# RMS norm and swish on one core: units of 8 rows in place of 4, and three pieces of work moved between engines

## The chip, the cores and the metric

The kernel runs on one core of a Trainium2 chip. The core has several engines, each with its own program: ScalarE (ACT in the profile), VectorE (DVE), GpSimd (POOL) and SyncE (SP) are used here; TensorE isn't. They work side by side and order themselves by semaphores. Data moves between the chip's memory (HBM) and the core's SBUF by DMA, which is started by an instruction on SyncE or ScalarE and then runs by itself on 16 DMA engines. [...]

The metric is the device time of one execution in microseconds. Before the change it is 161.33 us, the median of 3 runs from 159.96 to 161.42.

## The reference

```python
# x: 16 x 1024 x 512 float32; gamma: 512; eps = 1e-5
rms = np.sqrt(np.mean(x ** 2, axis=-1, keepdims=True) + eps)
x_norm = x / rms * gamma
return (x_norm * (1.0 / (1.0 + np.exp(-x_norm)))).astype(np.float32)
```

There are 16,384 rows of 512 numbers. Each row is scaled by one over its root mean square, multiplied by gamma, and passed through swish. 33.56 MB are read and as many written.

## The kernel before

**Rows and groups.** A "row" below means one row of x in each of the 128 partitions, so there are 128 of them, in four groups of 32. The buffer `xb` holds 96 rows; group 3 takes the place of group 0. All work on the rows is done in place. A load or store moves a piece of a group, given as (group, first row, rows).

**Loads** (line 117) are issued by SyncE in the order of the list `loads`. The first two are moved ahead of the start-up barrier (`early`). Loads of group 3 wait until the store of the piece that lay in the same place has landed.

**Stores** (line 191) are issued by ScalarE, inside its own program. A store waits for the swish of its last rows. `hold` makes stores 0 and 2 wait for a load as well, and gives the earliest place in ScalarE's program for them; so reads and writes mostly take turns: reads of groups 0 to 2, writes of group 0, reads of group 3, writes of groups 1 to 3.

**The work on a chunk of 4 rows**, k = 0 to 31:

- square(k), ScalarE: two row squares whose sum the engine accumulates itself (line 162, each followed by an instruction that reads the accumulator out), then one instruction that squares the other two rows into the PSUM buffer `sq` (line 169). A row square waits until the one two before it is done, by the semaphore `s_acc`.
- sums(k), VectorE: a reduction of `sq` to two row sums (line 215).
- GpSimd: adds eps (line 143) and raises to the power -0.5 (line 150).
- norm(k), VectorE: four instructions, each multiplies one row by its factor and by gamma (line 226).
- swish(k), ScalarE: one instruction over the four rows (line 181).

**The order on each engine is written out by hand.** ScalarE does square(k), then a store if one is due, then swish(k-2). VectorE does sums(k) and then norm(k-1). So norm(k-1) stands behind sums(k), which needs square(k), which may need a load.

At the start GpSimd clears three small tiles (lines 137 to 139). One of them is the buffer into which gamma is loaded; VectorE then spreads gamma over the partitions by a shuffle (line 239).

Of the kernel before, what the change touches and what calls it, by code (L numbers as in the profile page):

```python
# [9 lines left out]
def kernel(  # L10
# [7 lines left out]
    nc = tc.nc  # L18
    P = nc.NUM_PARTITIONS
    AF = mybir.ActivationFunctionType  # L20
    ALU = mybir.AluOpType
    fp32 = mybir.dt.float32
# [3 lines left out]
    R, D = xf.shape  # L26

    groups = [32] * 4
    slots = [0, 32, 64, 0]
    loads = [(0, 0, 4), (0, 4, 4), (0, 8, 8), (0, 16, 16), (1, 0, 32)]  # L30
    loads += [(2, 0, 28), (2, 28, 4), (3, 0, 28), (3, 28, 4)]
    stores = [(0, 0, 28), (0, 28, 4), (1, 0, 32), (2, 0, 32)]
    stores += [(3, 0, 16), (3, 16, 8), (3, 24, 8)]
    hold = {0: (loads.index((2, 0, 28)), 12), 2: (loads.index((3, 0, 28)), 22)}
    behind = {}
    ring = 96
    early = 2
    cn = 4
    n_sq = 2

    first = [sum(groups[:g]) for g in range(len(groups))]
    assert P * sum(groups) == R, R
# [1 line left out]

    chunks = []
    for i, (g, r, n) in enumerate(loads):
        for c in range(r, r + n, cn):
            chunks.append((slots[g] + c, i if c == r else None))
    K = len(chunks)
    assert K * cn * P == R  # L50

    ends = [-(-(first[g] + r + n) // cn) for g, r, n in stores]

    inv_d = 1.0 / float(D)
    eps_f = float(eps)
# [4 lines left out]
    def sbuf(name, shape, dt=fp32):  # L60
        return nc.alloc_sbuf_tensor(name, shape, dt).ap()

    xb = sbuf("xb", [P, ring, D])
    gamma4 = sbuf("gamma4", [P, D])
    gamma_sb = sbuf("gamma_sb", [P, D])
    neg_half = sbuf("neg_half", [P, cn])
    ms = sbuf("ms", [P, K, cn])
    aeps = sbuf("aeps", [P, K, cn])
    rstd = sbuf("rstd", [P, K, cn])
    sq = [nc.alloc_psum_tensor(f"sq{i}", [P, n_sq, D], fp32).ap() for i in range(2)]  # L70
    junk = [nc.alloc_psum_tensor(f"junk{i}", [P, D], fp32).ap() for i in range(2)]

    ld = [nc.alloc_semaphore(f"ld{t}") for t in range(len(loads))]
# [2 lines left out]
    blank = sbuf("blank", [P, 16])  # L76
    s_blank = nc.alloc_semaphore("s_blank")
    s_scratch = nc.alloc_semaphore("s_scratch")
    s_gld = nc.alloc_semaphore("s_gld")
    s_zero = nc.alloc_semaphore("s_zero")  # L80
    s_half = nc.alloc_semaphore("s_half")
    s_gamma = nc.alloc_semaphore("s_gamma")
    s_acc = nc.alloc_semaphore("s_acc")
    s_sq = nc.alloc_semaphore("s_sq")
    s_sum = nc.alloc_semaphore("s_sum")
    s_eps = nc.alloc_semaphore("s_eps")
    s_rstd = nc.alloc_semaphore("s_rstd")
    s_norm = nc.alloc_semaphore("s_norm")
    s_swish = nc.alloc_semaphore("s_swish")

    def need(ins, sem, value):
        return ins.wait_op(sem, value, "sem-ge")
# [30 lines left out]
    for t in range(early):  # L123
# [3 lines left out]
        at = next(  # L127
            i for i, other in enumerate(entry)
            if other.engine == mybir.EngineType.SP
            and isinstance(other, mybir.InstDrain)  # L130
        )
# [2 lines left out]
        load(t)  # L134
    nc.sync.wait_ge(s_scratch, 16)

    nc.gpsimd.memset(blank, 0.0).then_inc(s_blank, 1)  # L137
    nc.gpsimd.memset(gamma4, 0.0).then_inc(s_zero, 1)  # L138
    nc.gpsimd.memset(neg_half, -0.5).then_inc(s_half, 1)  # L139
    nc.gpsimd.wait_ge(s_half, 1)  # L140
    for k in range(K):
        need(
            nc.gpsimd.tensor_scalar(  # L143
                out=aeps[:, k, :], in0=ms[:, k, :], scalar1=eps_f, scalar2=None,
                op0=ALU.add,
            ),
            s_sum, k + 1,
        ).then_inc(s_eps, 1)
        need(
            nc.gpsimd.tensor_tensor(  # L150
                out=rstd[:, k, :], in0=aeps[:, k, :], in1=neg_half, op=ALU.pow
            ),
            s_eps, k + 1,
        ).then_inc(s_rstd, 1)

    def square(k):
        at, landing = chunks[k]
        if landing is not None:
            nc.scalar.wait_ge(ld[landing], 16)  # L159
        for j in range(n_sq, cn):  # L160
            n = k * (cn - n_sq) + j - n_sq
            acc = nc.scalar.activation(  # L162
                out=junk[n % 2], in_=xb[:, at + j, :], func=AF.Square,
                scale=inv_d**0.5, accum_out=ms[:, k, j : j + 1],
            )
            if n >= 2:
                need(acc, s_acc, n - 1)
            acc.then_inc(s_acc, 1)
        square = nc.scalar.activation(  # L169
            out=sq[k % 2], in_=xb[:, at : at + n_sq, :],  # L170
            func=AF.Square, scale=inv_d**0.5,
        )
        if k >= 2:
            need(square, s_sum, k - 1)
        square.then_inc(s_sq, 1)

    def swish(k):
        at, _ = chunks[k]
        rows = xb[:, at : at + cn, :]
        need(  # L180
            nc.scalar.activation(out=rows, in_=rows, func=AF.Silu), s_norm, k + 1  # L181
        ).then_inc(s_swish, 1)

    def after(t):
# [19 lines left out]
    for k in range(K + 3):  # L204
        if k < K:
            square(k)
        while stored < len(stores) and max(ends[stored] + 2, after(stored)) <= k:
            store(stored)
            stored += 1
        if 2 <= k < K + 2:  # L210
            swish(k - 2)

    def sums(k):
        need(
            nc.vector.tensor_reduce(  # L215
                out=ms[:, k, 0:n_sq], in_=sq[k % 2], op=ALU.add,
                axis=mybir.AxisListType.X,
            ),
            s_sq, k + 1,
        ).then_inc(s_sum, 1)  # L220

    def norm(k):
        at, _ = chunks[k]
        for j in range(cn):
            row = xb[:, at + j, :]
            ins = nc.vector.scalar_tensor_tensor(  # L226
                out=row, in0=row, scalar=rstd[:, k, j : j + 1], in1=gamma_sb,
                op0=ALU.mult, op1=ALU.mult,
            )
            if j == 0:  # L230
                need(ins, s_rstd, k + 1)
        ins.then_inc(s_norm, 1)

    for k in range(K + 1):
        if k < K:
            sums(k)
        if k == 0:
            need(
                nc.vector.stream_shuffle(gamma_sb, gamma4, [0] * 32), s_gld, 16  # L239
            ).then_inc(s_gamma, 1)  # L240
        if k == 1:
            nc.vector.wait_ge(s_gamma, 1)
        if k >= 1:
            norm(k - 1)
# [39 lines left out]
```

## Time and profile before

| What | Value |
|---|---|
| Median of 3 runs | 161.33 us |
| The profiled execution | 161.41 us |
| Its span in the profile | 160.1 us |
| Instructions in the span | 496 |
| Read, written | 33.56 MB, 33.56 MB |
| Mean transfer rate over the span | 419 GB/s |
| Busy: ScalarE, VectorE, GpSimd | 129.7, 124.4, 65.5 us |

The profile is of one execution. Its page gives the busy time of each engine, the span in 40 equal slices (each digit is a tenth of busy time, for DMA the mean share of the 16 DMA engines), the chain of work that ended last, and groups of like instructions. A line of a group reads: line of the kernel, engine, operation, output from inputs, shapes, count, then busy us in all and mean ns of one, then the idle time of the engine just before them, and what ended it. Longer views of the same trace list the instructions in order of time (start us, duration us, engine, line, operation) and the transfers that were issued in a stretch of time, with the us from issue to landing. "SPq" and "ACTq" mean the issuing of a transfer by SyncE or ScalarE.

### The profile page before, as it was taken

What the parts mean: (1) busy time and instruction counts of PE and PEld (TensorE: products, weight loads), DVE (VectorE), ACT (ScalarE), POOL (GpSimd) and SP (SyncE); (2) the same over time, 40 slices, a digit from 0 to 9 for tenths busy, and PEclk for the clock granted to TensorE, in tenths of its full rate; (3) what the DMA queues carried; (4) which work ended last, traced back from release to release, by engine and by line L of the source; (5) the groups of instructions that cost most, each with busy time, mean ns of one, the idle gap of its engine ahead of it and who ended that gap; (6) DMA issues with size and microseconds to landing.
All of it is one profiled execution on the core that took longest, in us unless ns stands there. A gap on an engine that the chain in (4) does not pass through costs nothing.

```text
span 160.1 us, 496 instructions
## 1 busy us (share of the span) xinstructions
DVE 124.4 (78%) x162; ACT 129.7 (81%) x193; POOL 65.5 (41%) x71
## 2 busy tenths in 40 slices
DVE  0239989999199998899999999999999999970000
ACT  0937989994799988999999999999999999571000
POOL 1035555555055555555555555555555555500000
DMA  7999996996999997999969996996996997899896
GB/s 264 458 461 393 450 598 262 524 524 262 458 461 446 444 411 338 458 458 458 450 258 458 458 458 266 518 524 278 508 508 297 508 475 327 385 426 483 368 426 270
DMA packets 2460, 67.16 MB, mean 419 GB/s; under 512 B 404, under 2 KB 404, under 8 KB 408
## 3 DMA queue, kind: packets, MB, share of 16 engines
q1 hardware_dynamic: 1296, 33.56, 49.4%
q10 hardware_dynamic: 1160, 33.57, 48.8%
q14 instruction: 4, 0.03, 0.0%
HBM read 33.56 MB, written 33.56 MB: 419 GB/s over the span
## 4 chain that ended last, share of the span: by engine, by line
ACT 55%; DMA 24%; DVE 7%; issue 3%; ACTq 1%; SPq 0%
ACT xb L181 24%; DMA xb<-in_x_dram 24%; ACT junk L162 18%; ACT sq L169 13%; DVE xb L226 5%; DVE ms L215 2%; ACTq L191 1%; SPq L117 0%; ACTq L159 0%
## 5 line engine op out<-in xcount | busy, mean ns | idle before, releaser
L226 DVE SCALAR_TENSOR_TENSOR xb<-xb,rstd,gamma_sb 128x512 f32<-128x512 f32 x128 | 87.3, 744 | 0.0
L181 ACT ACTIVATE xb<-xb 128x2048 f32<-128x2048 f32 x32 | 60.9, 1902 | 4.8 <-DVE xb L226 3.8
L215 DVE TENSOR_REDUCE ms<-sq 128x2 f32<-128x1024 f32 x32 | 39.2, 1223 | 16.1 <-ACT sq L169 13.1
L143 POOL TENSOR_SCALAR aeps<-ms 128x4 f32<-128x4 f32 x32 | 20.6, 644 | 70.0 <-DVE ms L215 70.0
L150 POOL TENSOR_TENSOR rstd<-aeps,neg_half 128x4 f32<-128x4 f32 x32 | 44.0, 1376 | 2.7
L162 ACT ACTIVATE junk<-xb 128x512 f32<-128x512 f32 x64 | 37.2, 582 | 6.7 <-DMA xb<-in_x_dram 6.6
L169 ACT ACTIVATE sq<-xb 128x1024 f32<-128x1024 f32 x32 | 32.1, 1005 | 0.0
L162 ACT ACTIVATION_READ_ACCUMULATOR junk<-xb 128x1 f32 x64 | 11.9, 186 | 0.0
L202 ACT ACT_TABLE_LOAD x1 | 1.3, 1283 | 3.6 <-issue 3.6
L239 DVE LOAD_MASK_SELECT gamma_sb<-gamma x1 | 0.0, 14 | 2.5 <-DMA gamma<-in_gamma_dram 2.5
L239 DVE STREAM_SHUFFLE gamma_sb<-gamma 128x512 f32<-128x512 f32 x1 | 0.7, 715 | 0.0
L137 POOL MEMSET blank<- 128x16 f32 x1 | 0.1, 111 | 1.5 <-POOLq L58 1.5
L138 POOL MEMSET gamma<- 128x512 f32 x1 | 0.5, 525 | 0.0
L265 POOL MEMSET const-float32-0.0<- 128x1 f32 x1 | 0.1, 98 | 0.2 <-issue 0.2
L265 POOL MEMSET const-bfloat16-1.0<- 128x1 bf16 x1 | 0.1, 102 | 0.0
L265 POOL MEMSET const-uint8-127<- 128x1 uint8 x1 | 0.1, 101 | 0.0
L139 POOL MEMSET neg_half<- 128x4 f32 x1 | 0.1, 101 | 0.0
L265 POOL MEMSET const-float32-1.0<- 128x1 f32 x1 | 0.1, 98 | 0.0
## 6 DMA issues: line engine op xcount, KB each, us to landing
xb<-in_x_dram SPq DMA_DIRECT2D x2, 7168.0 KB, 38.4
out_dram<-xb ACTq DMA_DIRECT2D x1, 7168.0 KB, 19.3
xb<-in_x_dram SPq DMA_DIRECT2D x4, 1024.0 KB, 14.0
xb<-in_x_dram SPq DMA_DIRECT2D x1, 4096.0 KB, 19.5
out_dram<-xb ACTq DMA_DIRECT2D x1, 4096.0 KB, 20.1
out_dram<-xb ACTq DMA_DIRECT2D x2, 2048.0 KB, 16.1
xb<-in_x_dram SPq DMA_DIRECT2D x1, 2048.0 KB, 10.2
out_dram<-xb ACTq DMA_DIRECT2D x1, 1024.0 KB, 21.3
```

What stands on the lines that cost most here:

```text
L138: nc.gpsimd.memset(gamma4, 0.0).then_inc(s_zero, 1)
L143: nc.gpsimd.tensor_scalar(out=aeps[:, k, :], in0=ms[:, k, :], scalar1=eps_f, scalar2=None, op0=ALU.add,),
L150: nc.gpsimd.tensor_tensor(out=rstd[:, k, :], in0=aeps[:, k, :], in1=neg_half, op=ALU.pow),
L162: acc = nc.scalar.activation(out=junk[n % 2], in_=xb[:, at + j, :], func=AF.Square, scale=inv_d**0.5, accum_out=ms[:, k, j : j + 1],)
L169: square = nc.scalar.activation(out=sq[k % 2], in_=xb[:, at : at + n_sq, :], func=AF.Square, scale=inv_d**0.5,)
L181: nc.scalar.activation(out=rows, in_=rows, func=AF.Silu), s_norm, k + 1
L191: nc.scalar.dma_start(out=dram(of, stores[t]), in_=buf(stores[t])),
L202: nc.scalar.preload_act_table_set("silu_and_others")
L215: nc.vector.tensor_reduce(out=ms[:, k, 0:n_sq], in_=sq[k % 2], op=ALU.add, axis=mybir.AxisListType.X,),
L226: ins = nc.vector.scalar_tensor_tensor(out=row, in0=row, scalar=rstd[:, k, j : j + 1], in1=gamma_sb, op0=ALU.mult, op1=ALU.mult,)
L239: nc.vector.stream_shuffle(gamma_sb, gamma4, [0] * 32), s_gld, 16
L265: nc = _bacc.Bacc("TRN2", target_bir_lowering=False, num_devices=1)
```

## The change

The unit of work becomes 8 rows, so that there are 16 units. In each:

- ScalarE accumulates three row sums itself and squares the other five rows in one instruction; the swish is one instruction over 8 rows.
- VectorE reduces five rows in one instruction. It also adds eps, in place, to all eight sums; this waits for the reduction by a semaphore.
- GpSimd does one power of 8 elements a partition, and nothing else.
- The buffer of the squares is in PSUM for even units and in SBUF for odd ones.
- The clearing of the small tiles goes from GpSimd to VectorE.
- Loads and stores are cut into pieces of 24 and 8 rows where they were 28 and 4, and the first load is of 8 rows in place of two of 4; the places in `hold` follow.

```diff
-    loads = [(0, 0, 4), (0, 4, 4), (0, 8, 8), (0, 16, 16), (1, 0, 32)]
-    loads += [(2, 0, 28), (2, 28, 4), (3, 0, 28), (3, 28, 4)]
-    stores = [(0, 0, 28), (0, 28, 4), (1, 0, 32), (2, 0, 32)]
+    loads = [(0, 0, 8), (0, 8, 8), (0, 16, 16), (1, 0, 32)]
+    loads += [(2, 0, 24), (2, 24, 8), (3, 0, 24), (3, 24, 8)]
+    stores = [(0, 0, 24), (0, 24, 8), (1, 0, 32), (2, 0, 32)]
     stores += [(3, 0, 16), (3, 16, 8), (3, 24, 8)]
-    hold = {0: (loads.index((2, 0, 28)), 12), 2: (loads.index((3, 0, 28)), 22)}
+    hold = {0: (loads.index((2, 0, 24)), 6), 2: (loads.index((3, 0, 24)), 11)}
...
-    cn = 4
-    n_sq = 2
+    cn = 8
+    n_sq = {8: 5}
...
-    sq = [nc.alloc_psum_tensor(f"sq{i}", [P, n_sq, D], fp32).ap() for i in range(2)]
+    sq = [
+        nc.alloc_psum_tensor("sq0", [P, n_max, D], fp32).ap(),
+        sbuf("sq1", [P, n_max, D]),
+    ]
...
-    nc.gpsimd.memset(blank, 0.0).then_inc(s_blank, 1)
-    nc.gpsimd.memset(gamma4, 0.0).then_inc(s_zero, 1)
-    nc.gpsimd.memset(neg_half, -0.5).then_inc(s_half, 1)
-    nc.gpsimd.wait_ge(s_half, 1)
-    for k in range(K):
-        need(
-            nc.gpsimd.tensor_scalar(
-                out=aeps[:, k, :], in0=ms[:, k, :], scalar1=eps_f, scalar2=None,
-                op0=ALU.add,
-            ),
-            s_sum, k + 1,
-        ).then_inc(s_eps, 1)
+    for k, (_, row, n, _) in enumerate(chunks):
         need(
             nc.gpsimd.tensor_tensor(
-                out=rstd[:, k, :], in0=aeps[:, k, :], in1=neg_half, op=ALU.pow
+                out=rstd[:, row : row + n], in0=ms[:, row : row + n],
+                in1=neg_half[:, :n], op=ALU.pow,
             ),
             s_eps, k + 1,
         ).then_inc(s_rstd, 1)
...
+    nc.vector.memset(blank, 0.0).then_inc(s_blank, 1)
+    nc.vector.memset(gamma4, 0.0).then_inc(s_zero, 1)
+    nc.vector.memset(neg_half, -0.5)
+
     def sums(k):
+        _, row, n, _ = chunks[k]
         need(
             nc.vector.tensor_reduce(
-                out=ms[:, k, 0:n_sq], in_=sq[k % 2], op=ALU.add,
-                axis=mybir.AxisListType.X,
+                out=ms[:, row : row + n_sq[n]], in_=sq[k % 2][:, : n_sq[n], :],
+                op=ALU.add, axis=mybir.AxisListType.X,
             ),
             s_sq, k + 1,
         ).then_inc(s_sum, 1)
+        need(
+            nc.vector.tensor_scalar(
+                out=ms[:, row : row + n], in0=ms[:, row : row + n],
+                scalar1=eps_f, scalar2=None, op0=ALU.add,
+            ),
+            s_sum, k + 1,
+        ).then_inc(s_eps, 1)
```

The order on ScalarE (square(k), store, swish(k-2)) and on VectorE (sums(k), now with the eps add, then norm(k-1)) is the same, with k counting units of 8 rows. In the built program store 3 stands behind square(14) and ahead of swish(12), as before it stood behind square(26) and ahead of swish(24).

More of the change, by code (lines that the diff above doesn't have):

```diff
@@ L46 @@
     for i, (g, r, n) in enumerate(loads):
-        for c in range(r, r + n, cn):
-            chunks.append((slots[g] + c, i if c == r else None))
-    K = len(chunks)
-    assert K * cn * P == R
-    ends = [-(-(first[g] + r + n) // cn) for g, r, n in stores]
+        while n:
+            m = min(n, cn)
+            start = slots[g] + r
+            row = chunks[-1][1] + chunks[-1][2] if chunks else 0
+            assert row == first[g] + r
+            chunks.append((start, row, m, i if start == slots[g] + loads[i][1] else None))
+            r, n = r + m, n - m
+    K = len(chunks)
+    rows = sum(n for _, _, n, _ in chunks)
+    assert rows * P == R
+    ends = []
+    for g, r, n in stores:
+        ends.append(
+            1 + next(k for k, c in enumerate(chunks) if c[1] + c[2] >= first[g] + r + n)
+        )
     inv_d = 1.0 / float(D)
@@ L66 @@
     neg_half = sbuf("neg_half", [P, cn])
-    ms = sbuf("ms", [P, K, cn])
-    aeps = sbuf("aeps", [P, K, cn])
-    rstd = sbuf("rstd", [P, K, cn])
-    sq = [nc.alloc_psum_tensor(f"sq{i}", [P, n_sq, D], fp32).ap() for i in range(2)]
+    ms = sbuf("ms", [P, rows])
+    rstd = sbuf("rstd", [P, rows])
+    n_max = max(n_sq.values())
+    sq = [
+        nc.alloc_psum_tensor("sq0", [P, n_max, D], fp32).ap(),
+        sbuf("sq1", [P, n_max, D]),
+    ]
     junk = [nc.alloc_psum_tensor(f"junk{i}", [P, D], fp32).ap() for i in range(2)]
@@ L80 @@
     s_zero = nc.alloc_semaphore("s_zero")
-    s_half = nc.alloc_semaphore("s_half")
     s_gamma = nc.alloc_semaphore("s_gamma")
@@ L154 @@
         ).then_inc(s_rstd, 1)
+    n_acc = 0
     def square(k):
-        at, landing = chunks[k]
+        nonlocal n_acc
+        at, row, n, landing = chunks[k]
         if landing is not None:
             nc.scalar.wait_ge(ld[landing], 16)
-        for j in range(n_sq, cn):
-            n = k * (cn - n_sq) + j - n_sq
+        for j in range(n_sq[n], n):
             acc = nc.scalar.activation(
-                out=junk[n % 2], in_=xb[:, at + j, :], func=AF.Square,
-                scale=inv_d**0.5, accum_out=ms[:, k, j : j + 1],
-            )
-            if n >= 2:
-                need(acc, s_acc, n - 1)
+                out=junk[n_acc % 2], in_=xb[:, at + j, :], func=AF.Square,
+                scale=inv_d**0.5, accum_out=ms[:, row + j : row + j + 1],
+            )
+            if n_acc >= 2:
+                need(acc, s_acc, n_acc - 1)
             acc.then_inc(s_acc, 1)
+            n_acc += 1
         square = nc.scalar.activation(
-            out=sq[k % 2], in_=xb[:, at : at + n_sq, :],
+            out=sq[k % 2][:, : n_sq[n], :], in_=xb[:, at : at + n_sq[n], :],
             func=AF.Square, scale=inv_d**0.5,
@@ L177, in swish @@
     def swish(k):
-        at, _ = chunks[k]
-        rows = xb[:, at : at + cn, :]
+        at, _, n, _ = chunks[k]
+        block = xb[:, at : at + n, :]
         need(
-            nc.scalar.activation(out=rows, in_=rows, func=AF.Silu), s_norm, k + 1
+            nc.scalar.activation(out=block, in_=block, func=AF.Silu), s_norm, k + 1
         ).then_inc(s_swish, 1)
@@ L220, in sums @@
         ).then_inc(s_sum, 1)
+        need(
[5 more added lines that the diff above has]
+        ).then_inc(s_eps, 1)
     def norm(k):
-        at, _ = chunks[k]
-        for j in range(cn):
-            row = xb[:, at + j, :]
+        at, row, n, _ = chunks[k]
+        for j in range(n):
+            x_row = xb[:, at + j, :]
             ins = nc.vector.scalar_tensor_tensor(
-                out=row, in0=row, scalar=rstd[:, k, j : j + 1], in1=gamma_sb,
-                op0=ALU.mult, op1=ALU.mult,
+                out=x_row, in0=x_row, scalar=rstd[:, row + j : row + j + 1],
+                in1=gamma_sb, op0=ALU.mult, op1=ALU.mult,
             )
```

## The prediction

> **What bounds the kernel now.** I read the page's totals first. No engine is full, but the DMA slices never fall below six tenths: the transfers run from start to end without a pause.
>
> ```profile
> DVE 124.4 (78%) x162; ACT 129.7 (81%) x193; POOL 65.5 (41%) x71
> ...
> DMA  7999996996999997999969996996996997899896
> ```
>
> Next, the chain that ended last. Its last 60 us are ScalarE and VectorE pieces and it stops at 144.9 us, 15 us before the end. So it doesn't show what sets the end. I asked for the transfers issued in the five short windows around the last five store issues (groups 1, 2 and three pieces of 3); the last figure of each line is us from issue to landing, and the first line below is an issue from the timeline.
>
> ```profile
> 114.28 0.34 ACTq L191 DMA_DIRECT2D out_dram<-xb  x1
> ...
> out_dram<-xb ACTq DMA_DIRECT2D x1, 21.8
> out_dram<-xb ACTq DMA_DIRECT2D x1, 26.4
> out_dram<-xb ACTq DMA_DIRECT2D x1, 4096.0 KB, 20.1
> out_dram<-xb ACTq DMA_DIRECT2D x1, 2048.0 KB, 17.0
> out_dram<-xb ACTq DMA_DIRECT2D x1, 2048.0 KB, 15.2
> ```
>
> With the issue times of the timeline (99.59, 114.28, 130.25, 138.23, 144.89) the landings are 121.4, 140.7, 150.35, 155.2 and 160.1. The steps between them are 19.3, 9.65, 4.85 and 4.85 us for 32, 16, 8 and 8 rows: 0.605 us a row each time. The stores stand in line behind each other, and each was issued before the one ahead had landed. **The write queue sets the end; the engines have slack against it.** How much? A 32-row transfer that finds the queues idle lands 21.8 us after its issue at the latest (store 2, which still shares with the last reads) and 19.36 + 1.2 = 20.6 at the least (0.605 x 32, plus start and completion, which I estimate at 1.2 from store 2's 21.8 - 19.36 = 2.4, halved). I take 21.2. Store 3, issued at 114.28, would then have landed by 135.5 alone and lands at 140.7: **5.2 us of slack**, the smallest of the last four (store 4: 16 rows, 9.7 + 1.8 alone, 8.6 us; stores 5 and 6: 10.3 and 8.5 us).
>
> Last, where the engines stand against that. ScalarE waits for the load of group 1 until 41.2 us, and after that it and VectorE run nearly without waiting.
>
> ```profile
> 41.22 0.60 ACT L162 ACTIVATE junk<-xb 128x512 f32<-128x512 f32 x1 [3.27 <-DMA xb<-in_x_dram]
> ...
> 43.50 1.23 DVE L215 TENSOR_REDUCE ms<-sq 128x2 f32<-128x1024 f32 x1 [3.52 <-ACT sq L169]
> 44.64 2.73 DVE L226 SCALAR_TENSOR_TENSOR xb<-xb,rstd,gamma_sb 128x512 f32<-128x512 f32 x4
> ...
> 112.36 1.89 ACT L181 ACTIVATE xb<-xb 128x2048 f32<-128x2048 f32 x1
> ```
>
> The four norms at 44.64 are the last of group 0; VectorE can't do them before the sum at 43.50, since sums(k) stands ahead of norm(k-1) in its program. The swish at 112.36 is the last of group 2, and store 3 goes out as it ends. So I time the changed kernel from 41.22 on, where the load releases it, up to store 3.
>
> **The change, part by part.** The durations are these (groups of the page):
>
> ```profile
> L226 DVE SCALAR_TENSOR_TENSOR xb<-xb,rstd,gamma_sb 128x512 f32<-128x512 f32 x128 | 87.3, 744 | 0.0
> L181 ACT ACTIVATE xb<-xb 128x2048 f32<-128x2048 f32 x32 | 60.9, 1902 | 4.8 <-DVE xb L226 3.8
> L215 DVE TENSOR_REDUCE ms<-sq 128x2 f32<-128x1024 f32 x32 | 39.2, 1223 | 16.1 <-ACT sq L169 13.1
> L143 POOL TENSOR_SCALAR aeps<-ms 128x4 f32<-128x4 f32 x32 | 20.6, 644 | 70.0 <-DVE ms L215 70.0
> L150 POOL TENSOR_TENSOR rstd<-aeps,neg_half 128x4 f32<-128x4 f32 x32 | 44.0, 1376 | 2.7
> L162 ACT ACTIVATE junk<-xb 128x512 f32<-128x512 f32 x64 | 37.2, 582 | 6.7 <-DMA xb<-in_x_dram 6.6
> L169 ACT ACTIVATE sq<-xb 128x1024 f32<-128x1024 f32 x32 | 32.1, 1005 | 0.0
> ```
>
> *ScalarE, a unit of 8 rows.* Two shapes of the same square (582 ns for 512, 1005 for 1024) give 0.83 ns an element and 0.16 us fixed. Three row squares at their pitch of 0.61 are 1.84; the square of 2560 is 1.005 + 1536 x 0.83 = 2.28; the swish of 4096 is 1.90 + 2048 x 0.83 = 3.60. Neighbours overlap by 0.09, so a unit is 7.55, against 2 x 4.0 = 8.0 before.
>
> *VectorE, a unit.* The sum of 2560 has no row. At most it is 2.5 x (1.223 - 0.08) + 0.08 = 2.94 (1.223 - 1.14, the part by which a sum overlaps the next instruction, isn't slope); at least 2.66 (if the 0.479 us between the 744 ns for 512 and the 1223 for 1024 is all slope). With the 0.16 us fixed of the square it is (1.223 - 0.16) x 2.5 + 0.16 = 2.82, which I take; every other one now reads SBUF, for which I have no other row. The eps add is new here: it waits for the sum's own semaphore (0.04 to 0.08, the gaps from a square to its sum and between GpSimd's pair), and lasts between 0.13 (a norm's 0.744 less 512 elements at the sum's 1.19 ns) and 0.23 (the first of GpSimd's own adds, at 8.50 us with VectorE idle; its 644 ns stand beside a busy VectorE, a cause that VectorE doesn't have to itself). I take 0.04 + 0.19, less 0.08 that the first norm overlaps it. Eight norms start 0.664 apart (5.31, the chain's last eight). Sum: 2.82 + 0.04 + 0.11 + 5.31 = **8.28** (8.06 to 8.48), against 2 x (1.14 + 2.66) = 7.6 before, where ScalarE's 8.0 set the pace. VectorE now sets it: from a swish's start, ScalarE has the next square ready in 3.51 + 1.84 + 2.28 + 0.04 = 7.67.
>
> [...] No row here shows a sum from SBUF.
>
> *The units' size, where group 0 meets the load of group 1.* The sum that stands ahead of group 0's last norms waits at 41.22 as before, but for three row squares and one of 2560: 41.22 + 1.84 + 2.28 + 0.04 gives 45.4 instead of 43.50. Norm(3) then ends 8.28 + 0.08 later, at 53.8; before, the same rows were done at 44.64 + 2.73 = 47.4. **6.4 us later.** Norm(11), the last of group 2, ends 8 units on: 53.8 + 66.2 = 120.0 (before 112.3). The swish of 8 rows ends at 120.05 + 3.6 = 123.65. Store 3 stands behind square(14) in ScalarE's program; before, such a store left while that square's instructions were still queued (114.28 against 115.38), so I let it leave early too, but the third row square now waits for the first: 0.7 more. Store 3 is issued at **124.4, 10.1 us later** than before, against 5.2 us of slack: the write queue runs dry and 4.9 us are lost.
>
> *What is hidden.* GpSimd: 32 adds and 16 powers go; a power of 8 costs 1.39 to 2.78, and norm(k) starts 5.3 us after its sum, behind norm(k-1); uncovered it would cost 2.8 once, at the end. The memsets on VectorE (0.53 on GpSimd) lie before its first sum at 7.19; gamma, which lands at 10.87, is not wanted before the first sum ends at 14.5. The first unit waits for 8 rows (7.2 instead of 4.9); VectorE is through norm(2) at about 42.6 and waits until 45.4 anyway; without that cover, 2.3. One load fewer on SyncE's queue: nothing, it is ahead. Pieces of 24 and 8 rows: load 4 lands four rows earlier, near 56.5; store 0 leaves at 53.8 + 3.65 + 0.7 = 58.1 (before 58.99), ahead of the last reads; store 2 follows norm(8) (95.2) at 99.5, as before (99.59). So the reads and the two turns keep their times. Stores 4 to 6 are ready at 140.3, 148.5 and 153.8 and need to be in line by about 143.8, 153.5 and 158.4.
>
> *Sum.* The span is 160.1 and the profiled execution 161.41, 0.08 above the median of 161.33; 1.3 lie outside the span. 161.4 + 4.9 = **166.3 us**.
>
> **The rivals.**
> 1. *Store 3 goes in program order, behind the whole square(14).* Its wait sits behind instructions with more waits than before. Then it leaves at 123.65 + 1.84 + 2.28 = 127.8: 3.4 more, 169.7. Against it: 114.28 above.
> 2. *Not slower: the sum costs little more than before.* If the sums that read SBUF ran at twice the rate, the mean sum would be 2.1 and VectorE's unit 7.58; ScalarE's 7.67 would then set the pace, store 3 would leave near 45.5 + 9 x 7.67 + 4.4 = 118.9 and be in line in time. It decides at a unit of about 7.75: 161.4. If the read stretch of the last loads (21.2 us for 32 rows, the stores 19.3) also shortened, 159.5. For it: ScalarE loses 0.45 us a unit. Against it: 2.66 as the least that the rows give a sum of 2560.
> 3. *The change doesn't do what it says:* if GpSimd's power of 8 took longer than the 5.3 us of cover, VectorE would wait for it each unit. Its row would have to quadruple for twice the elements. At 6.3 it would cost 9 x 1 = 9 us, 175.
>
> **How the numbers follow.** Forecast 0.80, rival 1 0.06, rival 2 0.11, rival 3 0.03. The unit's bounds make store 3 move by 9 x (-0.22, +0.20) = -2.0 to +1.8, the landing's by +-0.6: the range is 163.7 to 168.7, which leaves out the three rivals, 0.20. A measurement of this kernel can't tell 1% (1.6 us) from no change. Slower by more (over 162.9): 0.80 + 0.06 + 0.03 = 0.89; within 1%: 0.08; faster: 0.03, both from rival 2.
>
> **What would show it.** In the changed profile: the sum near 2.8 us and the eps add near 0.2; VectorE's units 8.3 apart, with little idle after 45; its busy time up to about 135 us; norm(3) ending near 53.8; store 3 issued near 124.4, and a hole in the DMA slices between 121 and 125. I am wrong if store 3 is issued before 120, or if the hole lies elsewhere (after 61 or after 102, at the two turns).

## The result and the profile after

The changed kernel takes 165.68 us (median of 4 runs, 165.61 to 165.71), the kernel before, measured beside it, 160.82 us (159.96 to 161.42). The ratio is 1.0305, with a 95% interval of 1.0248 to 1.0363: **slower by 3%**. The profiled execution of the changed kernel took 165.71 us with a span of 164.4, against 161.41 and 160.1 before: 4.3 us more in both.

The page of the changed kernel, its busy times and the DMA share and rate in 40 slices of 4.1 us:

```profile
DVE 132.8 (81%) x165; ACT 124.2 (76%) x129; POOL 32.9 (20%) x20
...
DMA  7999999699889899999999898999508999599897
GB/s 271 428 453 423 470 510 478 287 510 446 383 385 492 351 446 538 395 395 391 478 407 454 371 438 379 399 510 510 255 0 367 399 510 510 255 399 494 383 435 331
```

Before, the DMA engines paused nowhere. Now one slice is empty (the thirtieth, 119.2 to 123.3 us), and by the trace's packets nothing moves from 119.82 to 124.91. The slices count a packet where it starts: the last round of packets of store 2, 16 of 65,536 bytes, starts between 117.22 and 117.39 and ends by 119.82, and it is what the half-empty slice ahead of the hole (255) holds.

The same windows around the last five store issues as before; the first line is store 3's issue in the timeline, and the last figure of the others is us from issue to landing:

```profile
124.06 0.34 ACTq L196 DMA_DIRECT2D out_dram<-xb  x1
...
out_dram<-xb ACTq DMA_DIRECT2D x1, 20.7
out_dram<-xb ACTq DMA_DIRECT2D x1, 20.8
out_dram<-xb ACTq DMA_DIRECT2D x1, 4096.0 KB, 14.7
out_dram<-xb ACTq DMA_DIRECT2D x1, 2048.0 KB, 11.4
out_dram<-xb ACTq DMA_DIRECT2D x1, 2048.0 KB, 10.9
```

With the issues at 99.42, 124.06, 139.90, 148.13 and 153.43 the landings are, by the trace, 120.2, 144.9, 154.6, 159.5 and 164.4. The steps are 24.7, 9.7, 4.9 and 4.9 us, where they were 19.3, 9.7, 4.9 and 4.9. Only the first has changed, by 5.4 us. Store 2 landed 1.2 us earlier than before, and the later steps add 0.1: that is the 4.3 that the span shows.

The groups that set store 3's time:

```profile
L243 DVE SCALAR_TENSOR_TENSOR xb<-xb,rstd,gamma_sb 128x512 f32<-128x512 f32 x128 | 86.1, 747 | 0.0
L186 ACT ACTIVATE xb<-xb 128x4096 f32<-128x4096 f32 x16 | 57.8, 3615 | 13.5 <-DVE xb L243 13.5
L225 DVE TENSOR_REDUCE ms<-sq 128x5 f32<-128x2560 f32 x16 | 45.1, 2819 | 14.4 <-ACT sq L174 14.4
L151 POOL TENSOR_TENSOR rstd<-ms,neg_half 128x8 f32<-128x8 f32 x16 | 32.7, 2044 | 108.2 <-DVE ms L232 108.2
...
L174 ACT ACTIVATE sq<-xb 128x2560 f32<-128x2560 f32 x16 | 36.8, 2303 | 0.0
...
L232 DVE TENSOR_SCALAR ms<-ms 128x8 f32<-128x8 f32 x16 | 2.8, 172 | 0.5
```

And the chain that ended last, from the load of group 1 on (start us, us, what):

```profile
41.41 1.95 ACT junk L166 x6
43.36 2.20 ACT sq L174
45.56 0.02 issue
45.58 2.84 DVE ms L225
48.42 0.02 issue
48.44 0.17 DVE ms L232
48.61 5.29 DVE xb L243 x8
53.90 2.74 DVE ms L225
56.65 0.02 issue
56.67 0.17 DVE ms L232
56.84 5.29 DVE xb L243 x8
```

It goes on like this: VectorE without a gap, a unit each 2.74 + 0.02 + 0.17 + 5.29 = 8.23 us with rounding. ScalarE now waits for it (13.5 us ahead of the swishes, where before it was 3.8).

### The profile page after: what moved, and what is told of

Same layout as the page of the kernel before. It is cut to its first block, busy times and chain, and to the rows that moved or that the text cites. A ratio compares the mean times of both kernels' runs of the same rounds, so it can differ in the third digit from the quotient of the medians.

```text
span 164.4 us, 381 instructions
## 1 busy us (share of the span) xinstructions
DVE 132.8 (81%) x165; ACT 124.2 (76%) x129; POOL 32.9 (20%) x20
## 4 chain that ended last, share of the span: by engine, by line
DVE 63%; DMA 24%; ACT 5%; issue 0%; SPq 0%; ACTq 0%
DVE xb L243 42%; DMA xb<-in_x_dram 24%; DVE ms L225 20%; ACT xb L186 2%; ACT sq L174 1%; DVE ms L232 1%; ACT junk L166 1%; SPq L129 0%; ACTq L164 0%
## 5 line engine op out<-in xcount | busy, mean ns | idle before, releaser
L243 DVE SCALAR_TENSOR_TENSOR xb<-xb,rstd,gamma_sb 128x512 f32<-128x512 f32 x128 | 86.1, 747 | 0.0
L186 ACT ACTIVATE xb<-xb 128x4096 f32<-128x4096 f32 x16 | 57.8, 3615 | 13.5 <-DVE xb L243 13.5
L225 DVE TENSOR_REDUCE ms<-sq 128x5 f32<-128x2560 f32 x16 | 45.1, 2819 | 14.4 <-ACT sq L174 14.4
L151 POOL TENSOR_TENSOR rstd<-ms,neg_half 128x8 f32<-128x8 f32 x16 | 32.7, 2044 | 108.2 <-DVE ms L232 108.2
L166 ACT ACTIVATE junk<-xb 128x512 f32<-128x512 f32 x48 | 28.0, 583 | 11.9 <-DMA xb<-in_x_dram 11.9
L174 ACT ACTIVATE sq<-xb 128x2560 f32<-128x2560 f32 x16 | 36.8, 2303 | 0.0
L166 ACT ACTIVATION_READ_ACCUMULATOR junk<-xb 128x1 f32 x48 | 8.9, 186 | 0.0
L232 DVE TENSOR_SCALAR ms<-ms 128x8 f32<-128x8 f32 x16 | 2.8, 172 | 0.5
L219 DVE MEMSET gamma<- 128x512 f32 x1 | 0.5, 485 | 0.1
## 6 DMA issues: line engine op xcount, KB each, us to landing
out_dram<-xb ACTq DMA_DIRECT2D x2, 20.8
```

Of the source, the lines that this page charges most:

```text
L151: nc.gpsimd.tensor_tensor(out=rstd[:, row : row + n], in0=ms[:, row : row + n], in1=neg_half[:, :n], op=ALU.pow,),
L166: acc = nc.scalar.activation(out=junk[n_acc % 2], in_=xb[:, at + j, :], func=AF.Square, scale=inv_d**0.5, accum_out=ms[:, row + j : row + ...
L174: square = nc.scalar.activation(out=sq[k % 2][:, : n_sq[n], :], in_=xb[:, at : at + n_sq[n], :], func=AF.Square, scale=inv_d**0.5,)
L186: nc.scalar.activation(out=block, in_=block, func=AF.Silu), s_norm, k + 1
L219: nc.vector.memset(gamma4, 0.0).then_inc(s_zero, 1)
L225: nc.vector.tensor_reduce(out=ms[:, row : row + n_sq[n]], in_=sq[k % 2][:, : n_sq[n], :], op=ALU.add, axis=mybir.AxisListType.X,),
```

## The experiments

Each compares with the kernel before, run beside it on the same chip. The median of the kernel before was 159.81 us beside store 3 in two pieces, store 3 late, the pieces of 24 and 8 rows alone and four row sums; 160.45 beside the two versions with both stores cut, the one without the eps add and norm(3) first; 160.13 beside the kernel before with store 3 cut. "Theory" is that of the prediction: store 3 leaves too late, and the write queue runs dry. "Rival A" and "rival B" are those named in the first expectation, not rivals 1 to 3 of the prediction.

### Store 3 in two pieces

```diff
-    stores = [(0, 0, 24), (0, 24, 8), (1, 0, 32), (2, 0, 32)]
+    stores = [(0, 0, 24), (0, 24, 8), (1, 0, 32), (2, 0, 16), (2, 16, 16)]
```

> The changed kernel, with store 3 (32 rows of group 2) cut into two stores of 16 rows. Theory (store 3 is late, and the write queue runs dry from 119.8 to 124.9 us): the first half is ready after norm(9), 16.5 us before the second, and goes in line behind store 2; the second is issued at 124.1 as before and is not wanted before store 2 and the first half are through, near 130. The hole of 5.1 us goes whole; the span falls from 164.4 to 159.0 to 159.6, the time to 160.3 to 160.9. Rival A (the pieces of 24 and 8 rows, and reads and writes that overlap more, cost the time): no change, 165.7. Rival B (VectorE's longer units set the end by themselves): no change, 165.7.

Measured: 162.07 us (ratio 1.0128, 1.0079 to 1.0177). That is 3.6 us less than the changed kernel, with every compute instruction as it was. The hole at 120 is gone. But the time is 1.2 us above what the theory gave. The slices point to the place, and the packets say why:

```profile
DMA  7999996996999799999999979699699999599997
GB/s 265 446 468 391 473 571 261 522 522 261 465 503 404 336 550 408 391 404 416 485 404 440 514 322 485 261 522 522 261 391 522 391 391 473 236 465 391 391 457 326
```

The one slice at five tenths (236 GB/s) holds a second, small hole: by the packets nothing moves from 139.15 to 140.62. Store 4 waits for all its 16 rows and is issued at 139.78. In the changed kernel that store was in time only because store 3 was late. The expectation had filled one hole without asking which store comes next, though the prediction has the figure: store 4 had 8.6 us of slack, and it is 139.78 - 130.25 = 9.5 us late.

### Store 3 and store 4 in two pieces each

```diff
-    stores = [(0, 0, 24), (0, 24, 8), (1, 0, 32), (2, 0, 32)]
-    stores += [(3, 0, 16), (3, 16, 8), (3, 24, 8)]
+    stores = [(0, 0, 24), (0, 24, 8), (1, 0, 32), (2, 0, 16), (2, 16, 16)]
+    stores += [(3, 0, 8), (3, 8, 8), (3, 16, 8), (3, 24, 8)]
```

> The changed kernel with store 3 in two pieces of 16 rows, and store 4 in two of 8. With store 3 alone cut, the queue still ran dry once, from 139.2 to 140.6 us, since store 4 waited for all its 16 rows until 139.8. Theory: with its first half issued near 131.7 that hole goes too; the last store, issued at 153.3 as before and about 6 us long by itself, then comes within 0.5 us of setting the end: span 158.9 to 159.6, time 160.2 to 160.9. Rival B (VectorE's units set the end by themselves, through some other path): 162.1, as with store 3 alone cut.

Measured: 161.01 us, a ratio of 1.0021 (0.9994 to 1.0048): no difference from the kernel before can be seen, though the time is 0.1 above the range of the theory. No hole is left. The last store still leaves at 153.43, as in the changed kernel, and lands 5.2 us after the one ahead, where a queued store of 8 rows takes 4.9: it now sets the end, by 0.3 us. So the units of 8 rows, with VectorE's longer rounds, cost nothing measurable once the stores are cut to match; the loss that could be measured was in the write queue.

### The kernel before, with store 3 cut

```diff
-    stores = [(0, 0, 28), (0, 28, 4), (1, 0, 32), (2, 0, 32)]
+    stores = [(0, 0, 28), (0, 28, 4), (1, 0, 32), (2, 0, 16), (2, 16, 16)]
```

> The kernel before, with units of 4 rows and no hole in its write queue, and store 3 cut into two stores of 16 rows: the control for the same cut in the changed kernel. Theory (the cut there gained 3.6 us only by letting rows go out that were ready, into a queue that had run dry): nothing to gain here, 159.7 to 161.7, no difference from the kernel before. Rival (smaller stores are faster by themselves, whatever the hole): some us less, 156 to 158.

Measured: 160.21 us, ratio 0.9983 (0.9942 to 1.0025). Smaller stores gained nothing measurable here, where the queue never runs dry.

### The kernel before, with store 3 late

```diff
     ends = [-(-(first[g] + r + n) // cn) for g, r, n in stores]
+    ends[3] += 3
```

> The kernel before, with store 3 alone held back: it waits for the swish three chunks (12 rows) later than its own data, so that it is issued near 126.3 in place of 114.3, 12.0 us later; nothing else changes. Theory: 5.2 to 5.6 us of the 12.0 are slack, the rest is a hole in the write queue: 167.4 to 168.3 us. Rivals A and B: a store issued 12 us later, with all data ready and the engines unchanged, costs nothing or little: 161 to 163.

Measured: 168.44 us (ratio 1.0524, 1.0463 to 1.0586), 0.1 above the range. Nothing but one store was moved, and the loss is 1.8 times that of the change. Its rate over the slices shows the same hole, longer, from 119.16 to 127.61 by the packets:

```profile
GB/s 284 443 414 494 376 502 502 502 251 471 439 443 439 341 555 439 439 439 300 406 439 439 439 502 455 298 502 502 2 0 251 502 502 251 502 376 502 376 408 345
```

Store 3 went out at 126.78, and 12.0 us earlier its rows were ready. 168.44 - 159.81 = 8.6 of the 12.0 are lost, so the slack here was 3.4, less than the 5.2 of the prediction. In this execution store 2 landed at 120.0, in the profile that the prediction read at 121.3: that is 1.4 of the 1.8.

### The pieces of 24 and 8 rows alone

```diff
-    loads += [(2, 0, 28), (2, 28, 4), (3, 0, 28), (3, 28, 4)]
-    stores = [(0, 0, 28), (0, 28, 4), (1, 0, 32), (2, 0, 32)]
+    loads += [(2, 0, 24), (2, 24, 8), (3, 0, 24), (3, 24, 8)]
+    stores = [(0, 0, 24), (0, 24, 8), (1, 0, 32), (2, 0, 32)]
```

(and the indices in `hold`; the units stay at 4 rows)

> The kernel before, with units of 4 rows, but the loads and stores of groups 0, 2 and 3 cut into 24 and 8 rows as in the changed kernel. Theory: no hole, so no loss: 160.0 to 161.4; if the 1.7 us by which the last reads ended earlier in the changed kernel (100.0 against 101.7) come from the cut, the lower end. Rival A: most of the loss is here already, 163 to 166. Rival B: 161.4.

Measured: 160.43 us, ratio 1.0028 (1.0002 to 1.0053). At most half a per cent comes from the cut, so rival A falls.

### Four row sums on each engine

```diff
-    n_sq = {8: 5}
+    n_sq = {8: 4}
```

> The changed kernel, with four row sums on ScalarE and four on VectorE in place of three and five. Theory: VectorE's unit falls from 8.23 to 7.70 and ScalarE's round of 7.9 sets the pace; the first sum after the load starts 0.2 later, and store 3 stands behind one more row square (0.6). Store 3 near 121.7 in place of 124.1, the time 163.0 to 163.8. Rival A: 165.7. Rival B: 9 to 16 units of 0.33 each, 160.5 to 162.8.

Measured: 162.78 us (ratio 1.0175, 1.0125 to 1.0224); store 3 went out at 121.26. The sums take 2289 ns and start some 7.85 apart, ScalarE's round. The time lies just under the theory's range and at the edge of rival B's, so this run alone wouldn't tell them apart; store 3's issue and the two runs with cut stores do. The run also says where most of the delay comes from. With the row sums divided half and half, as in the kernel before, store 3 still leaves 121.26 - 114.28 = 7.0 us late of the 9.8: that part comes with the units of 8 rows (and the eps add), and 2.8 with the row sum that moved to VectorE.

### Without the eps add

```diff
-        need(
-            nc.vector.tensor_scalar(
-                out=ms[:, row : row + n], in0=ms[:, row : row + n],
-                scalar1=eps_f, scalar2=None, op0=ALU.add,
-            ),
-            s_sum, k + 1,
-        ).then_inc(s_eps, 1)
...
-            s_eps, k + 1,
+            s_sum, k + 1,
         ).then_inc(s_rstd, 1)
```

> The changed kernel without the eps add: it leaves out eps, and GpSimd's power waits for the sum itself. All else is the same. Theory: VectorE's unit falls from 8.23 to 8.04, nine of them lie ahead of store 3, which goes out 1.7 us earlier, near 122.3: 163.8 to 164.2. Rival (the add is hidden, or ScalarE's round sets the pace): 165.6.

Measured: 163.87 us (ratio 1.0191, 1.0145 to 1.0238). The sums start 8.03 apart, store 3 goes out at 122.20, 1.9 earlier, and the time is 1.8 less. An instruction of 0.17 us costs 0.2 in each of nine units, and all of it reaches the end.

### Norm(3) ahead of the sum that waits for the load

```diff
     for k in range(K + 1):
+        if k == 4:
+            norm(k - 1)
         if k < K:
             sums(k)
...
-        if k >= 1:
+        if k >= 1 and k != 4:
             norm(k - 1)
```

> The changed kernel with one change in VectorE's order: norm(3) stands ahead of sums(4), so it needn't wait for the load of group 1 and runs from 42.8 in the 2.8 us that VectorE idled. Theory in its refined form: ScalarE, released by the same load at 41.4, needs square(4), swish(2) and square(5) until 53.2 before VectorE can go on with sums(5), which began at 53.8; so only 0.6 of the 2.8 us comes through to store 3, and the time is 164.9 to 165.3. As the prediction tells it (the late norms alone carry the 6.4 us): store 3 goes 2.8 us earlier, 162.8 to 163.0.

Measured: 165.13 us (ratio 1.0270, 1.0214 to 1.0326), with store 3 at 123.26, 0.8 earlier. Of that, 0.16 is the load, which released ScalarE at 41.25 in place of 41.41 in this execution; the 0.6 that is left is what the refined form gave. This is VectorE and ScalarE's squares in that stretch, from the timeline:

```profile
45.33 3.60 ACT L186 ACTIVATE xb<-xb 128x4096 f32<-128x4096 f32 x1
47.83 2.82 DVE L225 TENSOR_REDUCE ms<-sq 128x5 f32<-128x2560 f32 x1
...
50.67 2.32 ACT L174 ACTIVATE sq<-xb 128x2560 f32<-128x2560 f32 x1
...
53.02 2.82 DVE L225 TENSOR_REDUCE ms<-sq 128x5 f32<-128x2560 f32 x1 [2.16 <-ACT sq L174]
```

VectorE has its norms done early and then stands idle for 2.16 us until square(5) is there; the sum that began at 53.82 begins at 53.02. So the loss at the load isn't VectorE's order alone: ScalarE, which the same load releases, has square(4), a swish of 8 rows and square(5) to get through first, and is nearly as late.

### Both cuts, and four row sums on each engine

```diff
-    stores = [(0, 0, 24), (0, 24, 8), (1, 0, 32), (2, 0, 32)]
-    stores += [(3, 0, 16), (3, 16, 8), (3, 24, 8)]
+    stores = [(0, 0, 24), (0, 24, 8), (1, 0, 32), (2, 0, 16), (2, 16, 16)]
+    stores += [(3, 0, 8), (3, 8, 8), (3, 16, 8), (3, 24, 8)]
...
-    n_sq = {8: 5}
+    n_sq = {8: 4}
```

> The same two cuts, with four row sums on ScalarE and four on VectorE. Theory: the last store is issued at 148.95 in place of 153.3 and has slack again; with no hole left the 96 rows of the last writes run from 99.5 to 158.0, and the time is that of the kernel before or a little less: 159.3 to 160.2. Rival B: 161 or more, since each unit is still as long as in the run with four and four.

Measured: 161.32 us (160.66 to 161.78), ratio 1.0036 (1.0002 to 1.0069). The time is 1.1 us above the expected range: the last store leaves at 148.84 with slack, there is no hole, and the time isn't less than with five sums on VectorE. What ends late here is described below under the hardware. No version beat the kernel before.

### One line through the runs

In the five kernels where store 3 leaves a hole, the time of the profiled execution follows the issue of store 3 in it:

| Kernel | Store 3 issued | Time of the same execution | Difference |
|---|---|---|---|
| four and four | 121.26 | 162.91 | 41.65 |
| without the eps add | 122.20 | 163.85 | 41.65 |
| norm(3) first | 123.26 | 164.92 | 41.66 |
| the changed kernel | 124.06 | 165.71 | 41.65 |
| before, store 3 late | 126.78 | 168.43 | 41.65 |

Over 5.5 us of issue time, with units of 4 and 8 rows, the difference stays within 0.01. Of the 41.65, 20.8 are store 3 itself, 19.5 the 32 rows behind it, and 1.3 lie outside the span.

## Why the prediction was right

The time was forecast as 166.3 and measured as 165.68; the direction, the place and the cause hold. Step by step, predicted and then measured in the changed kernel's profile:

| Step | Predicted | Measured |
|---|---|---|
| Sum of five rows, eps add | 2.82, 0.19 us | 2.82, 0.17 us |
| VectorE's unit | 8.28 us | 8.23 us |
| First sum after the load | 45.4 | 45.58 (the load released ScalarE at 41.41, not 41.22) |
| norm(3) ends | 53.8 | 53.90 |
| norm(11) ends | 120.0 | 119.8 |
| Store 2 issued | 99.5 | 99.42 |
| Store 3 issued | 124.4 | 124.06 |
| Store 3 from issue to landing | 21.2 | 20.8 |
| Stores 4, 5, 6 issued | 140.3, 148.5, 153.8 | 139.90, 148.13, 153.43 |
| Power of 8 on GpSimd | 1.39 to 2.78 | 2.04, hidden |

**The bound.** Reading the landings in place of the chain of waits was the step that mattered. That chain ends at the last swish in both kernels and shows neither the queue nor the hole. The cut stores show that the queue is the cause, and the late store in the kernel before shows that it suffices.

**The time and the slack.** In the time itself the slack cancels. 166.3 is store 3's issue (124.4), its 21.2, the 19.4 of the rows behind it and 1.3 outside the span; measured were 124.06, 20.8, 19.5 and 1.3. The slack decides the loss against the kernel before, and there it was the term that was off in size. It was read as 5.2 us from one execution, in which the last load completed over 2.2 us (one of its 16 completions 1.7 behind the others) and store 2 landed at 121.3. In the changed kernel store 2 landed at 120.2, in the kernel with the late store at 120.0. The slack by medians is 9.8 (store 3's delay, 124.06 - 114.28) - 4.9 = 4.9 for the change, and 3.4 by the late store. That the loss of 4.9 between the medians is just the one forecast is partly luck: the forecast started from 161.4, the slowest of the four executions of the kernel before (159.96 to 161.42), and against that one the loss is 4.3.

**The load.** "6.4 us later" at norm(3) is right as a time (53.90 - 47.37 = 6.5). Its telling wasn't: the prediction put it on the sum that stands ahead of the norms. With the order changed, 0.6 us of the 2.8 that VectorE idles came back. The rest is held by ScalarE and the length of its own units.

**ScalarE's program.** Store 3 left just after the second of three row squares had begun, as the prediction had it, 0.65 after the swish ended:

```profile
119.79 3.62 ACT L186 ACTIVATE xb<-xb 128x4096 f32<-128x4096 f32 x1 [0.55 <-DVE xb L243]
...
123.93 0.58 ACT L166 ACTIVATE junk<-xb 128x512 f32<-128x512 f32 x1
124.06 0.34 ACTq L196 DMA_DIRECT2D out_dram<-xb  x1
...
125.15 2.29 ACT L174 ACTIVATE sq<-xb 128x2560 f32<-128x2560 f32 x1
```

Rival 1 would have put it behind the square, at 127.4 by the trace. It fell.

**The other rivals.** Rival 2 needed a unit of 7.75 us, so a mean sum of about 2.3; its own assumption, sums from SBUF at twice the rate, gave 2.1. The sums of even units read PSUM, those of odd units SBUF; all sixteen lie between 2.810 and 2.827, so nothing like twice the rate shows. Squares into PSUM took 2.28 us and into SBUF 2.32, 0.04 that ScalarE had to spare. Rival 3 needed a power above 5.3 us; it took 2.04.

**Fewer instructions.** There are 381 in place of 496, and ScalarE's busy time fell by 5.5 us and GpSimd's by half. ScalarE's gain had no use, as VectorE became the slower of the two: its busy time rose by 8.4 us.

## What to carry to other kernels

Where transfers follow each other without a pause, work out for each store when it must be in line, from the landing of the one ahead, and compare that with when its last row is ready; the smallest of these margins is what a change may cost before it shows (here store 3 was 9.8 us late and 4.9 were lost), and the margin of the next store tells what remains once the first is mended (here store 4 was 9.5 us late against 8.6). Units of 8 rows, with the eps add, put store 3 off by 7.0 us here, and the row sum that moved to VectorE by 2.8 more, so the store's pieces have to be chosen with the units: with units of 8 rows and stores of 32 the kernel lost 3%, with stores of 16 and 8 nothing that could be measured. The instruction count said little here, 381 in place of 496; the engine that became the slower one, and the queue behind it, decided.

## What was not expected of the hardware

**In the table below, the completions of a store came apart by up to 2.49 us, and behind a hole they lay within 0.23.** A store's semaphore counts 16 completions, taken here as one for each engine. The time between the first and the last of them, in us, from the trace (of a store in pieces, the last piece):

| Kernel | Store 2 | Store 3 | Last store | Hole ahead of store 3 |
|---|---|---|---|---|
| before | 1.17 | 1.10 | 0.99 | none |
| before, store 3 cut | 0.89 | 1.05 | 0.96 | none |
| both cuts, four and four | 2.46 | 2.49 | 2.43 | none |
| both cuts | 0.64 | 0.48 | 0.17 | none |
| four and four | 2.38 | 0.23 | 0.21 | 121.1 to 122.1 |
| before, store 3 late | 1.10 | 0.19 | 0.19 | 119.2 to 127.6 |
| changed | 0.18 | 0.23 | 0.19 | 119.8 to 124.9 |

In the kernel with both cuts and four row sums, the last load already completes over 2.58 us, and each store from there on over 2.4 to 2.5. In each of these stores the last completion comes 1.0 us after the next to last: if each is one engine's, one engine is late and stays late, and the kernel waits for it. That would account for the 1 to 2 us by which the run missed its expectation. Where the queue ran dry ahead of store 3, the spread went: from 2.38 to 0.23 with four and four, from 1.10 to 0.19 with the late store. Behind the hole of the changed kernel the 16 first packets of store 3 start within 0.14 us, from 124.91 to 125.05. There the spread had gone before the hole already, at the turn from reads to writes: the last load completes over 1.17 us, store 2 over 0.18. Store 2's 16 first packets start between 100.26 and 100.41, as the last completion of that load comes in (100.35).

The runs' scatter fits: 160.66 to 161.78 with both cuts and four sums, and 159.58 to 161.92 in the kernel before, beside the experiments; against 165.61 to 165.71 in the changed kernel, and 160.88 to 161.12 with both cuts alone. With one profile of each kernel this link isn't shown. In all these kernels the group 1 load still completes within 0.6 us, and the spread is 0.9 to 1.5 us in the next load (near 57). Why a completion falls behind there wasn't tried and stays open.

**GpSimd's power took less than twice as long for twice the elements**: 1.38 us for 4 elements a partition, 2.04 for 8. In the run with norm(3) first, the one of 8 that had VectorE idle beside it took 1.64.
